# A two-layer decoder trunk: when the weights of the last feed-forward block are prepared, and three smaller reorderings

## The chip, the cores and the metric

The program runs on one core of a Trainium2 chip. Its engines are TensorE (PE: matmuls, with its weight loads listed apart as PEld), VectorE (DVE), ScalarE (ACT), GpSimd (POOL), and SyncE (SP), which here only issues transfers. Each works through its own queue in order; 16 DMA engines carry what SP, ACT and POOL issue. The metric is the time of one execution in microseconds (us) of device time. Three runs of the kernel before took 1037.97, 1039.06 and 1039.12 us: the median is 1039.06.

## The reference, cut to what matters

The input x has 256 rows (the sequence) of 1024 numbers; c is one row that conditions all. Two layers each do

```
x = x + 0.5 * gate0 * swiglu_ffn(pre(x, 0), w_in[i, 0], w_out[i, 0])
x = x + gate1 * mixer(pre(x, 1))            # layer 0: attention, layer 1: convolution module
x = x + 0.5 * gate2 * swiglu_ffn(pre(x, 2), w_in[i, 1], w_out[i, 1])
pre(z, j) = rms_norm(z, norm_g[i, j]) * (1 + scale_j) + shift_j
shift, scale, gate = (silu(c) @ ada_w[i] + ada_b[i]) cut into pieces
swiglu_ffn(h, w_in, w_out): a, b = split(h @ w_in); (silu(a) * b) @ w_out      # 2 x 2816 columns
```

The attention has 16 heads of 64, with q and k normalized by head, a distance penalty and a causal mask. The convolution module is

```
a, g = split(h @ w_pw1 + b_pw1); u = a * sigmoid(g)
u = depthwise causal convolution of width 31 over the rows, one filter for each of the 1024 channels
u = silu(layer_norm(u)) @ w_pw2 + b_pw2
```

All is float32: some 250 MB of weights are read once.

## The kernel before, in words

The 256 rows are two tiles, t = 0 and t = 1, of 128. Every large product is made in three matmuls (`mm3`, lines 680 to 682): each operand is a high part in a format that TensorE takes at full rate, and the rest as a low part; high x high, high x low and low x high are summed.

**The stream of weights.** All weights form one list, in the order of use, of pieces of 512 KB (`raw`), held in six buffers. `step()` takes the next piece: ACT copies the high part (`whi`, L251, one piece ahead), DVE subtracts it to get the low part (`wlo`, L226), the buffer comes free, and SP issues the load of the piece six places later (L211). Pieces of `ada_w` are instead summed up by DVE with the weights silu(c) (`acc`, L290 and L292). Two pieces are a unit, and high and low parts of six units fit (`RING`); a piece of a seventh is refused until the oldest unit has had its last use. Who calls `step()`: `need(unit)` until the unit is there; `block()` ahead of each group of matmuls, which adds a quota (`take(n)` sets it, about 1.6 to 1.8 here, 0 to stop) to a credit and steps as often as that holds a whole number; and explicit calls. As every queue is in order, the place of a `step()` in the program is its place among the other work of DVE and ACT.

**The feed-forward blocks** (`ffn`): for each of 11 chunks of 256 columns, U(t, c, u) makes the up products, `gate` silu(a) * b, `TR` turns it by transposes (L763) and splits it into gh and gl (L771, L772), and Dn(t, c) adds its part of the down product into y[t], two banks of 512 columns. `residual` (L614, L617) adds y to x, in the last block in pieces of 512, 256 and 256 columns, each stored at once. Between blocks `residual` also makes the norm: squares (ACT), a power (POOL), the scaled rows z (DVE); `turn` then transposes z (L659), applies scale and shift (hf, L665 and L667) and splits the result into hh and hl (L674, L675), which the next block's U products need.

**The start.** For each of four quarters q of the channels `early_sum` sums ada_w for the first scale and shift: one-column matmuls of acc (L544), sums of raw pieces (L554), a copy by ACT (`br`, L560), and one-column matmuls of it (L563); `early_transposes` turns the rows (L588). For q = 0 idle matmuls (L448) on constants fill waits.

**The attention** (`attention`): the order is written out in one list. U: q, k or v products; R, N, Q: norm of q and k and their transposes; S: scores of two heads (PE), penalty and row minimum (DVE L908), exponentials (ACT L914); M: division by the sum (DVE, L923 and L925); X: transposes of the result (PE, L932); V: product with v.

**The convolution** (`conv`): the channels are eight groups b of 128. U(b) makes the two halves, `glu(b)` multiplies them into a buffer ub (ACT L1085, DVE L1086). `park(b)` (POOL, L1095) writes ub to DRAM and `spread(b)` (POOL, L1103) reads it back in four transfers in a layout R in which 32 channels stand at four shifts; `wide(b)` (L1039) builds the matching filter matrix wd, on POOL or, for b of 6 and 7, on DVE. C(b) (L1111) is the depthwise product: 64 matmuls on R and wd, and a copy of the result by ACT (`v`, L1115). C(6) and C(7) are made in two halves, for the rows of t = 0 and of t = 1. `VT` transposes v, bn_stats and `norm` make the layer norm, `swish` and `put` the operand of O(t, j), the last product of the module, over four units of w_pw2. After it come `residual`, `turn` and the last feed-forward block. In the loop over b, `steps` says how many pieces are taken behind each C(b): 2, 2, 2 and 1 behind C(0) to C(3).

Of the kernel before, what the change touches and what calls it, by code (L numbers as in the profile page):

```python
# [14 lines left out]
P = 128  # L15
D = 1024
# [3 lines left out]
NC = DFF // 256  # L20
# [8 lines left out]
IDLE_START = 20  # L29
IDLE_SUMS = 2  # L30
IDLE_FOLD = 9
IDLE_PICK = 2
IDLE_FIRST = 12
MASKED = 1e30


# [22 lines left out]
class Trunk:  # L59
# [213 lines left out]
    def take(self, n=None):  # L273
        self.quota = PUMP[self.phase] if n is None else n
# [263 lines left out]
    def early_sum(self, q, acc, shift, idle):  # L538


        nc = self.nc
        def scale(ps):
            for i in range(2):
                nc.tensor.matmul(ps[:, i : i + 1], acc[:, i * P : i * P + P], self.one, start=True, stop=True)  # L544

        rows = self.bank("m" if q else "y")
        if not q:
            ps = self.bank("m")
            scale(ps)
        for e, raw in enumerate(shift):  # L550
            if not q and not e:
                idle(IDLE_SUMS)
            for k in range(4):
                nc.tensor.matmul(  # L554
                    rows[32 * k : 32 * k + 32, 0:256], self.sc32[:, 4 * e + k, :], raw[:, k, :],
                    start=e == 0, stop=e == 1,
                )
            self.issue()
        br = self.two.tile([P, 256], F32, name="br", tag="sq", bufs=1)
        nc.scalar.activation(br, rows[:, 0:256], AF.Copy)  # L560
        def shifts(ps):
            for i in range(2):
                nc.tensor.matmul(ps[:, 2 + i : 3 + i], br[:, i * P : i * P + P], self.pick, start=True, stop=True)  # L563

        if q:
            pt = self.early_transposes(q)
            ps = self.bank("m")
            scale(ps)
            shifts(ps)
        else:  # L570
            idle(IDLE_PICK)
            shifts(ps)
            pt = self.early_transposes(q)

        def fin():
            for j, kind in enumerate((1, 0)):
                self.finish(self.vecs[0, 0, kind], ps[:, 2 * j : 2 * j + 2], q * 256, 2)

        return fin, pt
# [112 lines left out]
            self.mm3(ps, self.hh[:, kk, ts], self.hl[:, kk, ts], unit.hi[:, cs], unit.lo[:, cs], kk == 0, kk == 7)  # L692
        unit.uses -= 1

    def rows256(self, y, lh, ll, unit, first, last, mid=None, quarters=False):


        self.need(unit)
        self.block()
        for h in range(2):  # L700
            if h and mid:
                mid()
            n = 256 if h and quarters else 512
            for o in range(0, 512, n):
                for k in range(2):
                    cs = slice(k * D + h * 512 + o, k * D + h * 512 + o + n)
                    self.mm3(
                        y[h][:, o : o + n], lh(k), ll(k), unit.hi[:, cs], unit.lo[:, cs],
                        first and k == 0, last and k == 1 and o + n == 512,
                    )  # L710
        unit.uses -= 1

    def bank(self, tag):
# [6 lines left out]
    def ffn(self, i, l, s, before, after, first=None, last=False, mid=None):  # L720
# [4 lines left out]
        up, down = p["up"], p["down"]  # L725
# [10 lines left out]
        def U(t, c, u):  # L736
            if u == 0:
                us[t, c] = self.bank("u")
            self.cols512(us[t, c], t, up[c][u], u)
            if u == 1:  # L740
                gate(t, c)
# [15 lines left out]
        def TR(c, ts=(0, 1)):  # L757
            ps = self.bank("m")
            g = gs[c]
            for j, t in enumerate(ts):  # L760
                for k in range(2):
                    o = (2 * j + k) * P
                    nc.tensor.transpose(ps[:, o : o + P], g[:, t, k * P : k * P + P], self.ident)  # L763
            if c not in gts:
                gts[c] = [
                    self.fp.tile([P, 2, 256], F32R, name=n, tag=n, bufs=3) for n in ("gh", "gl")
                ]
            n = len(ts)
            hi, lo = (gt[:, ts[0] : ts[0] + n, :] for gt in gts[c])
            src = ps[:, 0 : n * 256].rearrange("p (t n) -> p t n", t=n)  # L770
            nc.scalar.activation(hi, src, AF.Copy)  # L771
            nc.vector.tensor_tensor(lo, src, hi.bitcast(F32), op=ALU.subtract)  # L772

        def Dn(t, c, mid=None, quarters=False):
            if t not in y:
                y[t] = self.new_y()
            hi, lo = gts[c]
            self.rows256(
                y[t], lambda k: hi[:, t, k * P : k * P + P], lambda k: lo[:, t, k * P : k * P + P],
                down[c], c == 0, c == NC - 1, mid, quarters,  # L780
            )

        if first:
            self.take()
# [9 lines left out]
        else:  # L794
            take = self.take
# [8 lines left out]
        for c in range(6 if first else 2, e):  # L804
            U(0, c, 0), U(1, c, 0), TR(c - 1)
            if c == 7 and mid:
                mid()
            U(0, c, 1), U(1, c, 1)
            Dn(0, c - 1), Dn(1, c - 1)
        take = self.take  # L810
        U(0, e, 0), TR(e - 1), U(0, e, 1), Dn(0, e - 1), TR(e, (0,)), U(1, e, 0)
        self.need(down[e])
# [1 line left out]
        Dn(0, e)  # L814
        g2 = self.vecs[l, s, 2].out
        self.residual(0, y[0], g2, 0.5, last)
        take(0), U(1, e, 1), take(1), Dn(1, e - 1), TR(e, (1,))
        after()
        Dn(1, e, None, last)
        self.residual(1, y[1], g2, 0.5, last)  # L820


# [18 lines left out]
    def attention(self, ap, before, after):  # L841
# [3 lines left out]
        def U(t, units, u):  # L845
            if u == 0:
                us[t, id(units)] = self.bank("y")
            self.cols512(us[t, id(units)], t, units[u], u)
# [124 lines left out]
        U(1, A, 1), Q(0, 0), U(1, v0, 0), R(1, 0), U(1, v0, 1), N(1, 0)  # L973
        U(0, B, 0), Q(1, 0), W(1, 0), U(0, B, 1), S(0)
        U(1, B, 0), R(0, 1), M(0), U(1, B, 1), N(0, 1)
        U(0, C, 0), X(0), S(1), R(1, 1), Q(0, 1), U(0, C, 1), M(1), V(0), N(1, 1)
        U(1, C, 0), X(1), R(0, 2), Q(1, 1), U(1, C, 1), V(1), N(0, 2), S(2)
        U(0, E, 0), R(1, 2), Q(0, 2), M(2), U(0, E, 1), N(1, 2), X(2), S(3)
        U(1, E, 0), R(0, 3), Q(1, 2), V(2), M(3), U(1, E, 1), N(0, 3), X(3), S(4)
# [40 lines left out]
    def conv(self, cp, before, after):  # L1020
# [71 lines left out]
        def park(b):  # L1092

            drams[b] = self.dram.tile([P, 288], F32, name=f"d{b}")
            nc.gpsimd.dma_start(drams[b], ub[b % 4])  # L1095
# [107 lines left out]
        take(PUMP_LOOP)  # L1203
        U(4)
        glu(4)
        steps = (2, 2, 2, 1, 0, 0)
        for b in range(4):
            if b < 3:
                U(b + 5)
            if b == 0:  # L1210
                take(0)
            park(b + 4), spread(b + 3)
            if b:
                wide(b + 2)
            if b < 3:
                glu(b + 5)
            C(b)
            for _ in range(steps[b]):
                self.step()
            if b:  # L1220
                VT(b - 1)
                if b == 1:
                    nc.vector.tensor_tensor(b2, b2, gate, op=ALU.mult)
                else:
                    x = self.x[b - 2]
                    nc.vector.tensor_tensor(x, x, b2, op=ALU.add)
        nc.scalar.activation(warm, self.mhalf, AF.Silu)
        spread(7), wide(6, nc.vector)
        C(4)
        for _ in range(steps[4]):  # L1230
            self.step()
        VT(3), wide(7, nc.vector)
        C(5)
        for _ in range(steps[5]):
            self.step()
        VT(4), C(6, 0, P), VT(5), take(4), self.block(), C(7, 0, P), VT(6, (0,))
        take(0)
        C(6, P, P), VT(7, (0,)), moments(0), norm(0, 0), norm(0, 1)
# [66 lines left out]
```

## Time and profile before

| | us |
|---|---|
| median of three runs | 1039.06 |
| the profiled execution | 1036.53 |
| its span, first to last instruction | 1034.7 |
| PE, PEld busy | 1016.2, 824.0 |
| DVE, ACT, POOL busy | 785.9, 490.1, 71.3 |
| mean granted TensorE clock | 0.997 of full |

Times are counted from the first instruction. A busy PE in the table is not a PE at its peak: matmuls overlap, and the ends are modelled. So the stretches in which the next matmul waits for another engine, and their releaser, say more than the share. The stages in this execution: the start to about 60 us, the first feed-forward block to 228, the attention to 337, two feed-forward blocks to 735, the convolution with its last product to 842, the last block to the end.

### The profile page before, as it was taken

What the parts mean: (1) busy time and instruction counts of PE and PEld (TensorE: products, weight loads), DVE (VectorE), ACT (ScalarE), POOL (GpSimd) and SP (SyncE); (2) the same over time, 40 slices, a digit from 0 to 9 for tenths busy, and PEclk for the clock granted to TensorE, in tenths of its full rate; (3) what the DMA queues carried; (4) which work ended last, traced back from release to release, by engine and by line L of the source; (5) the groups of instructions that cost most, each with busy time, mean ns of one, the idle gap of its engine ahead of it and who ended that gap; (6) DMA issues with size and microseconds to landing.
All of it is one profiled execution on the core that took longest, in us unless ns stands there. A gap on an engine that the chain in (4) does not pass through costs nothing.

```text
span 1034.7 us, 14612 instructions
## 1 busy us (share of the span) xinstructions
PE 1016.2 (98%) x5457; PEld 824.0 (80%) x5457; DVE 785.9 (76%) x1167; ACT 490.1 (47%) x762; POOL 71.3 (7%) x123
## 2 busy tenths in 40 slices
PE   9999999999999999999999999999999899999998
PEld 6788787887676888887888887888986788888886
DVE  5779888988897788878778778786788578656633
ACT  4554344566575544444455444354534356444420
POOL 3000000002210000000020000000166000000000
PEclk9999999999999999999999999999999899999999
DMA  9989999948665399999839889886599238766601
GB/s 334 331 272 340 315 328 322 321 145 274 233 216 194 107 328 318 298 318 306 298 101 310 287 301 302 286 291 198 173 279 312 97 104 304 233 214 218 219 32 41
DMA packets 183754, 256.08 MB, mean 247 GB/s; under 512 B 9045, under 2 KB 132726, under 8 KB 183684
## 3 DMA queue, kind: packets, MB, share of 16 engines
q1 hardware_dynamic: 180928, 248.55, 72.3%
q0 software_dynamic: 2608, 6.55, 2.3%
q8 instruction: 43, 0.70, 0.3%
q14 instruction: 27, 0.22, 0.1%
q10 hardware_dynamic: 148, 0.06, 0.0%
HBM read 252.89 MB, written 2.23 MB: 247 GB/s over the span
## 4 chain that ended last, share of the span: by engine, by line
PE 86%; DVE 7%; ACT 3%; DMA 3%; issue 1%; POOL 0%; SPq 0%; DVEq 0%; ACTq 0%; POOLq 0%
PE u L682 15%; PE u L680 15%; PE u L681 15%; PE y L680 11%; PE y L682 11%; PE y L681 11%; PE m L1111 2%; DVE wlo L226 2%; PE m L763 2%; DVE acc L292 2%; DMA raw<-in_ada_w_dram 1%; DMA R<-d 1%; ACT whi L251 1%; ACT p L914 1%; DMA raw<-in_attn_w_qkv_dram 1%
## 5 line engine op out<-in xcount | busy, mean ns | idle before, releaser
L226 DVE TENSOR_TENSOR wlo<-raw,whi 128x1024 fp32r<-128x1024 f32 x320 | 386.0, 1235 | 32.4 <-ACT whi L251 32.3
L251 ACT ACTIVATE whi<-raw 128x1024 fp32r<-128x1024 f32 x320 | 329.3, 1055 | 155.5 <-DMA raw<-in_ffn_w_in_dram 73.0
L680 PE MATMUL u<-whi,hh 128*128 128x512 f32 x672 | 266.3, 396 | 0.0
L682 PE MATMUL u<-whi,hl 128*128 128x512 f32 x672 | 262.8, 391 | 0.1
L681 PE MATMUL u<-wlo,hh 128*128 128x512 f32 x672 | 261.8, 390 | 0.2 <-DVE wlo L226 0.2
L292 DVE SCALAR_TENSOR_TENSOR acc<-raw,sc,acc 128x512 f32<-128x512 f32 x224 | 172.2, 769 | 5.1
L682 PEld LDWEIGHTS u<-whi,hl 128*128 128x128 f32 x672 | 126.1, 188 | 29.1 <-DVE hl L604 1.4
L680 PEld LDWEIGHTS u<-whi,hh 128*128 128x128 f32 x672 | 126.2, 188 | 26.2 <-issue 0.8
L681 PEld LDWEIGHTS u<-wlo,hh 128*128 128x128 f32 x672 | 126.4, 188 | 25.7 <-DVE wlo L226 0.6
L680 PE MATMUL y<-whi,gh 128*128 128x512 f32 x354 | 138.5, 391 | 0.7 <-ACT gh L771 0.7
L682 PE MATMUL y<-whi,gl 128*128 128x512 f32 x354 | 137.6, 389 | 0.0
L681 PE MATMUL y<-wlo,gh 128*128 128x512 f32 x354 | 137.4, 388 | 0.0
L772 DVE TENSOR_TENSOR gl<-m,gh 128x512 fp32r<-128x512 f32 (+1 forms) x48 | 31.0, 647 | 88.9 <-ACT gh L771 88.7
L680 PE MATMUL y<-whi,hh 128*128 128x512 f32 (+1 forms) x256 | 96.7, 378 | 1.5 <-DVE hh L1164 0.8
L682 PE MATMUL y<-whi,hl 128*128 128x512 f32 (+1 forms) x256 | 93.9, 367 | 0.0
L681 PE MATMUL y<-wlo,hh 128*128 128x512 f32 (+1 forms) x256 | 93.6, 366 | 0.0
L771 ACT ACTIVATE gh<-m 128x512 fp32r<-128x512 f32 (+1 forms) x48 | 27.0, 563 | 135.2 <-PE m L763 135.1
L733 ACT ACTIVATE sg<-u 128x256 f32<-128x256 f32 x84 | 32.1, 383 | 110.4 <-PE u L682 110.4
L680 PEld LDWEIGHTS y<-whi,gh 128*128 128x128 f32 x354 | 66.5, 188 | 16.3 <-ACT gh L771 1.4
L682 PEld LDWEIGHTS y<-whi,gl 128*128 128x128 f32 x354 | 66.5, 188 | 14.5 <-DVE gl L772 0.6
L681 PEld LDWEIGHTS y<-wlo,gh 128*128 128x128 f32 x354 | 66.5, 188 | 13.4
L680 PEld LDWEIGHTS y<-whi,hh 128*128 128x128 f32 x256 | 48.7, 190 | 12.5 <-issue 3.5
(178 smaller groups left out, 881.7 us busy)
## 6 DMA issues: line engine op xcount, KB each, us to landing
raw<-in_ffn_w_in_dram SPq DMA_DIRECT2D x164, 512.0 KB, 5.2
raw<-in_ada_w_dram SPq DMA_DIRECT2D x144, 512.0 KB, 5.0
raw<-in_ffn_w_out_dram SPq DMA_DIRECT2D x88, 512.0 KB, 5.1
raw<-in_attn_w_qkv_dram SPq DMA_DIRECT2D x24, 512.0 KB, 5.1
raw<-in_conv_w_pw_dram SPq DMA_DIRECT2D x24, 512.0 KB, 6.1
raw<-in_ffn_w_in_dram SPq DMA_DIRECT2D x24, 256.0 KB, 4.7
R<-d POOLq DMA_DIRECT2D x32, 142.0 KB, 7.3
raw<-in_attn_w_o_dram SPq DMA_DIRECT2D x8, 512.0 KB, 4.2
```

The costliest lines, as they stand in the source:

```text
L226: (eng or nc.vector).tensor_tensor(lo, raw, hi.bitcast(F32), op=ALU.subtract)
L251: self.nc.scalar.activation(hi, self.like(self.raws[i], hi), AF.Copy)
L292: nc.vector.scalar_tensor_tensor(dst, raw[:, i, :], self.sc[:, k : k + 1], dst, op0=ALU.mult, op1=ALU.add)
L680: nc.tensor.matmul(out, lh, rh, start=start, stop=False)
L681: nc.tensor.matmul(out, lh, rl, start=False, stop=False)
L682: nc.tensor.matmul(out, ll, rh, start=False, stop=stop)
L733: nc.scalar.activation(sg, ps[:, 0:256], AF.Silu)
L763: nc.tensor.transpose(ps[:, o : o + P], g[:, t, k * P : k * P + P], self.ident)
L771: nc.scalar.activation(hi, src, AF.Copy)
L772: nc.vector.tensor_tensor(lo, src, hi.bitcast(F32), op=ALU.subtract)
L914: nc.scalar.activation(p[:, c0:c1], p[:, c0:c1], AF.Exp, bias=st[:, t : t + 1], scale=-1.0, accum_out=st[:, 2 + t : 3 + t],)
L1111: nc.tensor.matmul(ps[32 * g : 32 * g + 32, :], wd[b][:, q, g, :], R[b][:, g, 4 * q + t0 : 4 * q + t0 + n], start=q == 0, stop=q == 7,)
```

## The change

There are four parts. **Convolution**: the list `steps` is gone; no piece is taken behind C(0) to C(3), two are taken behind C(5) instead. `wide(4)` stands on POOL ahead of park(6) and spread(5) instead of behind them. **Last feed-forward block**: the down products of t = 1 for the last three chunks are made by columns. The second 512 columns of chunk 8 are left for the end, then the first 512 columns are finished, and the second 512 in two pieces of 256 with the last two chunks each. **Attention**: M(1) stands right behind S(1), ahead of R(1,1), Q(0,1) and U(0,C,1), instead of behind them. **Start**: for q = 0 the transposes stand ahead of the one-column matmuls of br, in place of two idle matmuls, and 8 instead of 12 idle matmuls follow.

```diff
-IDLE_PICK = 2
-IDLE_FIRST = 12
+IDLE_FIRST = 8
...
+        pt = self.early_transposes(q)
         if q:
-            pt = self.early_transposes(q)
             ps = self.bank("m")
             scale(ps)
-            shifts(ps)
-        else:
-            idle(IDLE_PICK)
-            shifts(ps)
-            pt = self.early_transposes(q)
+        shifts(ps)
...
+        def Dp(c, o, n, last=False):
+            hi, lo = gts[c]
+            self.need(down[c])
+            for k in range(2):
+                cs, gs_ = slice(k * D + o, k * D + o + n), slice(k * P, k * P + P)
+                self.mm3(
+                    y[1][o // 512][:, o % 512 : o % 512 + n], hi[:, 1, gs_], lo[:, 1, gs_],
+                    down[c].hi[:, cs], down[c].lo[:, cs], False, last and k == 1,
+                )
...
-            Dn(0, c - 1), Dn(1, c - 1)
+            Dn(0, c - 1)
+            if last and c == e - 1:
+                Dp(e - 2, 0, 512)
+            else:
+                Dn(1, c - 1)
...
-        take(0), U(1, e, 1), take(1), Dn(1, e - 1), TR(e, (1,))
-        after()
-        Dn(1, e, None, last)
+        take(0), U(1, e, 1), take(1)
+        if last:
+            Dp(e - 1, 0, 512), TR(e, (1,)), Dp(e - 2, 512, 512), Dp(e, 0, 512, True)
+            for o in (512, 768):
+                Dp(e - 1, o, 256), Dp(e, o, 256, o == 768)
+        else:
+            Dn(1, e - 1), TR(e, (1,))
+            after()
+            Dn(1, e)
...
-        U(0, C, 0), X(0), S(1), R(1, 1), Q(0, 1), U(0, C, 1), M(1), V(0), N(1, 1)
+        U(0, C, 0), X(0), S(1), M(1), R(1, 1), Q(0, 1), U(0, C, 1), V(0), N(1, 1)
...
-        steps = (2, 2, 2, 1, 0, 0)
         for b in range(4):
             if b < 3:
                 U(b + 5)
             if b == 0:
                 take(0)
+            if b == 2:
+                wide(4)
             park(b + 4), spread(b + 3)
-            if b:
+            if b in (1, 3):
                 wide(b + 2)
             if b < 3:
                 glu(b + 5)
             C(b)
-            for _ in range(steps[b]):
-                self.step()
...
         C(5)
-        for _ in range(steps[5]):
-            self.step()
+        self.step(), self.step()
         VT(4), C(6, 0, P), VT(5), take(4), self.block(), C(7, 0, P), VT(6, (0,))
```

## Rows read from the trace of the kernel before

**Rows 1.** The page, part 1: busy us, share of the span, instructions by engine.

```profile
PE 1016.2 (98%) x5457; PEld 824.0 (80%) x5457; DVE 785.9 (76%) x1167; ACT 490.1 (47%) x762; POOL 71.3 (7%) x123
```

**Rows 2.** Windows by stage; after each engine's busy us: PEclk, DMA share, GB/s.

```profile
790.00:815.00 25.00, 20.14 (x411) 14.75 (x411) 15.74 (x17) 8.28 (x13) 6.57 (x10) 0.93 0.82 247
815.00:835.00 20.00, 19.21 (x88) 15.73 (x88) 12.13 (x30) 9.03 (x22) 1.10 (x2) 0.91 0.00 1
835.00:862.00 27.00, 27.00 (x128) 22.35 (x127) 22.57 (x35) 17.48 (x30) 0.55 (x1) 1.00 0.51 165
900.00:950.00 50.00, 50.00 (x228) 41.32 (x227) 29.93 (x34) 20.77 (x26) 0.00 (x0) 1.00 0.68 219
```

**Rows 3.** Timeline of PE, last depthwise products: start, duration, [idle before <- releaser].

```profile
798.93 1.96 PE L1111 MATMUL m<-R,wd 128*32 128x128 f32 x64 [0.75 <-DMA R<-d]
...
805.36 2.77 PE L1111 MATMUL m<-R,wd 128*32 128x128 f32 x64 [4.10 <-DMA R<-d]
...
811.27 1.95 PE L1111 MATMUL m<-R,wd 128*32 128x128 f32 x64
...
816.99 0.80 PE L680 MATMUL y<-whi,hh 128*128 128x512 f32 x1 [0.79 <-DVE hh L1164]
```

**Rows 4.** Timeline of POOL, 764 to 798 us.

```profile
782.68 0.60 POOL L1095 DMA_DIRECT2D d<-ub  x1 [1.78 <-DMA d<-ub]
...
787.50 0.60 POOL L1095 DMA_DIRECT2D d<-ub  x1
...
791.69 2.12 POOL L1039 TENSOR_TENSOR wd<-w,mask 128x1024 f32<-128x1024 f32 x1
795.29 2.21 POOL L1103 DMA_DIRECT2D R<-d  x4 [1.48 <-issue]
```

**Rows 5.** Tile R, then loads by line (KB, median us to landing), 740:815 and 860:1000.

```profile
DMA to landing us min/median/max: 5.4/7.3/9.4
...
raw<-in_ffn_w_in_dram SPq DMA_DIRECT2D x8, 512.0 KB, 14.2
...
raw<-in_ffn_w_in_dram SPq DMA_DIRECT2D x31, 512.0 KB, 5.0
```

**Rows 6.** Window 817 to 820 us, columns as in Rows 2.

```profile
817.00:820.00 3.00, 3.00 (x7) 2.42 (x8) 2.90 (x8) 1.71 (x5) 0.13 (x1) 0.50 0.00 0
```

**Rows 7.** Timeline of DVE from O(0,3) to the first chunk, then PE's there.

```profile
829.25 0.69 DVE L614 SCALAR_TENSOR_TENSOR tmp<-y,gate 128x512 f32<-128x512 f32 x1 [1.76 <-PE y L682]
...
836.50 1.37 DVE L665 TENSOR_SCALAR hf<-m,mod,mod 128x128 f32<-128x128 f32 x4 [0.61 <-PE m L659]
...
840.21 3.49 DVE L226 TENSOR_TENSOR wlo<-raw,whi 128x1024 fp32r<-128x1024 f32 x3
843.61 0.68 DVE L614 SCALAR_TENSOR_TENSOR tmp<-y,gate 128x512 f32<-128x512 f32 x1
...
854.43 0.50 PE L682 MATMUL u<-whi,hl 128*128 128x512 f32 x1
```

**Rows 8.** Timeline of ACT and of PE's weight loads at the start.

```profile
25.78 1.06 ACT L251 ACTIVATE whi<-raw 128x1024 fp32r<-128x1024 f32 x1 [0.25 <-DMA raw<-in_ffn_w_in_dram]
...
28.47 0.19 PEld L680 LDWEIGHTS u<-whi,hh 128*128 128x128 f32 x1 [0.33 <-ACT hh L603]
```

**Rows 9.** Timeline of PE and DVE in the attention, around M(1) and X(1).

```profile
267.25 1.27 PE L932 MATMUL m<-ident,p 128*128 128x128 f32 x6 [1.70 <-DVE p L925]
...
263.23 0.69 DVE L856 TENSOR_REDUCE s<-sq 128x8 f32<-128x512 f32 x1 [1.51 <-ACT sq L853]
...
267.93 0.68 DVE L864 TENSOR_TENSOR z<-y,r 128x512 f32<-128x512 f32 x1
```

**Rows 10.** Timeline of PE and DVE at the end of the kernel.

```profile
1026.97 0.50 PE L680 MATMUL y<-whi,gh 128*128 128x512 f32 x1 [0.47 <-ACT gh L771]
...
1030.18 0.42 DVE L614 SCALAR_TENSOR_TENSOR tmp<-y,gate 128x256 f32<-128x256 f32 x1
...
1031.56 0.42 DVE L617 TENSOR_TENSOR x<-x,tmp 128x256 f32<-128x256 f32 x1
```

More of the change, by code (lines that the diff above doesn't have):

```diff
@@ L693, in cols512, with rows256 @@
         unit.uses -= 1
-    def rows256(self, y, lh, ll, unit, first, last, mid=None, quarters=False):
+    def rows256(self, y, lh, ll, unit, first, last, mid=None):
         self.need(unit)
@@ L702, in rows256 @@
                 mid()
[L703 to L710, printed above, removed]
+            for k in range(2):
+                cs = slice(k * D + h * 512, k * D + h * 512 + 512)
+                self.mm3(y[h], lh(k), ll(k), unit.hi[:, cs], unit.lo[:, cs], first and k == 0, last and k == 1)
         unit.uses -= 1
@@ L772, in TR, with Dn @@
             nc.vector.tensor_tensor(lo, src, hi.bitcast(F32), op=ALU.subtract)
-        def Dn(t, c, mid=None, quarters=False):
+        def Dn(t, c, mid=None):
             if t not in y:
@@ L779, in Dn @@
                 y[t], lambda k: hi[:, t, k * P : k * P + P], lambda k: lo[:, t, k * P : k * P + P],
-                down[c], c == 0, c == NC - 1, mid, quarters,
+                down[c], c == 0, c == NC - 1, mid,
             )
+        def Dp(c, o, n, last=False):
+            hi, lo = gts[c]
+            self.need(down[c])
+            for k in range(2):
+                cs, gs_ = slice(k * D + o, k * D + o + n), slice(k * P, k * P + P)
[3 more added lines that the diff above has]
+                )
         if first:
@@ L1229, in conv @@
         C(4)
-        for _ in range(steps[4]):
-            self.step()
         VT(3), wide(7, nc.vector)
         C(5)
-        for _ in range(steps[5]):
-            self.step()
+        self.step(), self.step()
         VT(4), C(6, 0, P), VT(5), take(4), self.block(), C(7, 0, P), VT(6, (0,))
```

## The prediction, made before the changed kernel ran

> **What bounds the kernel now.** First the busy shares: PE is busy for 98% of the span, DVE for 76% [rows 1]. That says where to look, not what a stage waits for, so next the windows by stage. In the last block, 900 to 950 us, PE runs without a gap, 228 matmuls in 50 us or 0.22 us each, and DVE is idle for 40% of it: PE alone sets the pace, and whatever comes late or early there is passed to the end unchanged [rows 2]. The end of the convolution, 790 to 815, is different: PE is busy for 20.1 of 25 us and its clock is 0.93 of full. Behind it, 815 to 835, no DMA moves at all and DVE is idle for 7.9 of 20 us; from 835 to 862 DVE is busy for 22.6 of 27 [rows 2]. Third, the timeline of PE in the bad stretch: C(6) for t = 0 waits 0.75 us for R, C(7) for t = 0 waits 4.10 us, and then 64 matmuls take 2.77 instead of 1.95 us, because the clock has fallen [rows 3]. So this stage is bound by the last spread, not by PE. I follow what each part does to the start of O(0,0), now at 816.99, and then to the stages behind it.
>
> **Convolution, the depthwise products.** The chain that ends last is POOL's. park(6) is issued at 782.68 after POOL was idle for 1.78, so POOL was free at 780.9; park(7) goes out at 787.50; wide(5) ends at 791.69 + 2.12 = 793.81; spread(7), which needs the landing of d(7), starts at 795.29, 7.8 us after park(7) [rows 4]. Afterwards wide(4) starts at 780.9, in that idle time, and park(6) behind it at about 783.0, 0.3 late. park(7) no longer has wide(4) ahead of it and its input no longer stands behind DVE's pieces: 785.7, 1.8 early. With the same 7.8 us d(7) has landed by 793.5; wide(5) still ends near 793.8. So spread(7) starts at about 793.8, 1.5 early. Its last transfer went out three quarters through the four, at 796.95, and PE started at 805.36, 8.4 later. A transfer of R took 5.4 at best, 7.3 in the middle and 9.4 at worst, while a load of 512 KB beside it took 14.2 against 5.0 in the last block [rows 5]: the two share the engines. With the loads gone (six stay in flight until about 787) I take the best value: 793.8 + 1.65 + 5.4 + 0.2 = 801.0. C(6), without its wait, would let PE go on at 800.4, so C(7) starts at 801.0.
>
> From there: three half products of 1.9 at full clock and two pairs of transposes of 0.2 end at about 807.2 (before: 805.36 to 811.27 + 1.95 = 813.22). In this time ACT meets four copies of weight pieces ahead of its copy of C(7); at 1.06 each they end about when PE needs it, and I charge 0.1. From the end of the last half product to O(0,0) it was 816.99 - 813.22 = 3.8 [rows 3], the same work after: O(0,0) at 811.1, **5.9 us earlier**. Ends: if R stays as slow as before (8.4), C(7) starts at 803.9 and the gain is 3.1; with no wait at all it is 6.5.
>
> **The clock.** Between 817 and 820 PE made 7 matmuls in 3.00 us at 0.50 of the clock, 0.43 each, against 0.22 [rows 2, 6]: 7 x 0.21 = 1.5 us, say 1.4. That fall came after 3.8 us of narrow products and transposes, with only 0.79 of idle time [rows 3]. The same work stands ahead of O(0,0) afterwards. Whether the clock falls again depends on when the chip looks, which one trace can't show: 0 or 1.4, I take **0.7 gained**. The Trainium skill ("TensorE: Matmul & The Clock Gate", section "Why this matters for your kernels") ties a return to the lower level to idle gaps of PE between bursts of matmuls. By that rule nothing would fall here afterwards and the term would be 1.4; the row, a fall with next to no gap, speaks for 0; the middle stands.
>
> **The pieces that were put off.** Five of the seven pieces of `steps` now come later: they fall into the O stage, where before the ring of six units was full and no piece could be taken. Counting the credits with 1.6 for each group of O: two pieces ahead of O(0,2), one ahead of O(0,3), two ahead of O(1,0), one, two and two ahead of the next three. So by the end of the module 21 pieces are done, against 20 before, and the first sum of ada_w also comes one group sooner. A piece is 1.16 us of DVE (3.49 for three) [rows 7]. Where do they stand? Three between the last `put` and residual(0): DVE was idle 1.76 there, until 829.25, so residual(0) moves by 3.5 - 1.8 = 1.7. Three instead of one ahead of hf at 836.50, where 0.61 was idle: hf moves by 1.7 + 2.3 - 0.6 = 3.4, of which the wait for hh takes up some 0.6: 2.8. Four instead of three ahead of residual(1), which followed the pieces without a gap (840.21 + 3.49, 843.61): 2.8 + 1.2 = 4.0. Then z, the transposes, hf and hl of t = 1 follow, with the early sum of ada_w another 0.3: 4.3 to 4.5. PE needed that hl at 854.43, when it was just there, its matmul lengthened to 0.50 [rows 7]. So PE loses **4.4 us**, in pieces at O(0,3), the transposes of t = 1 and U(1,0,0). Ends: 0, if five pieces (5.8) fit into the 7.9 idle us [rows 2]; 8.1, if seven stand on the path in full. The chain in rows 7 is in order and had no slack at its end, so I take the worked value. The loads behind these pieces find idle DMA engines [rows 2] and cost nothing; were they as slow as 14.2 [rows 5], rival B would hold.
>
> **Start.** Six idle matmuls less, at 0.23 some 1.4 us of PE, let the first products begin up to 0.7 earlier (they then wait for hh and hl of the first quarter). But in the second quarter ACT waits for a load until 25.78, and its copy of 1.06 stands ahead of hf and hh, for which PE waits at 28.47 [rows 8]. PE only waits longer: **0**. Ends: 0.7 gained; 1.4 lost if the thinner start costs the clock one fall.
>
> **Attention.** X(1) waits 1.70 for M(1) [rows 9]. Put behind S(1), M(1) falls into the 1.51 us in which DVE waits for ACT's square at 263.23, and pushes that a little. What is late next is z at 267.93, which stood behind M(1) and which the next transposes need as soon as X(1) ends, 267.25 + 1.27; it moves by the length of M(1), about 1.3, less 0.3. I take **1.0**; ends 0 (DVE waits for the exponentials as long as it gained) and 1.7.
>
> **Tail.** The wait of 0.47 for gh goes, since twelve other matmuls lie between TR and its use, and the first matmul's restart (0.50 for 0.23) with it; six matmuls of 512 columns become twelve of 256, about 0.07. Behind the last matmul DVE needs 1030.18 to 1031.56 + 0.42, 1.80 us for four operations [rows 10]. Both pieces lie in one bank, and residual stands behind all their matmuls, so I take it that this stays: **0.7** gained. Ends 0.5 and, if the first piece needn't wait, 1.7. The deferral of chunk 8 itself moves no work off PE.
>
> **Sum.** 5.9 + 0.7 - 4.4 + 0 + 1.0 + 0.7 = 3.9 us. The profiled execution took 1036.53 (span 1034.7 and 1.8 around it): 1032.6. The median of the runs is 2.5 higher, 1039.06, and is what is compared: **1035.2**.
>
> **Rivals.**
> A. The put-off pieces are absorbed: DVE finds the idle time in front of each step of the chain, 4.4 becomes 0. Time 1035.2 - 4.4 = 1030.8. For it: 7.9 idle us between 815 and 835. Against: that idle time lies ahead of waits on PE, in order, and 835 to 862 has only 4.4 [rows 2].
> B. A load stands in ACT's queue. The copy of the sixth piece after the two steps behind C(5) needs a load that is issued only at about 798, and ACT's copy of C(7) stands behind it. I reckon with 5 us [rows 5]; at 7.4 it is 2.4 late, and so is O(0,0): 1037.6.
> C. The slower side: spread(7) isn't freed. If R(7) is paced by its own small packets and by the landing of d(7), C(7) starts near 805 as before, 5.9 and the 0.7 of the clock are gone, and the put-off pieces are paid all the same: 1035.2 + 6.6 = 1041.8. It decides from a start of C(7) at about 804. For it: the median of 7.3 is the same while loads come and go. Against: the spread of 5.4 to 9.4 [rows 5]. The Trainium skill ("DMA: Bandwidth & Descriptors", "Queues, rings and completion order") has each DMA engine take turns between the queues that have work; by that rule an empty load queue must shorten R, and C would fail.
>
> **How the numbers follow.** Two runs of this kernel can't be told apart within some 0.2%, 2.1 us. My forecast, a loss of 3 to 6 at the pieces and C(7) before 802, holds 1032.5 to 1037.0: chance 0.46. A 0.16, B 0.14, C 0.13; 0.11 is left for small terms that leave it within 0.2%. Faster: 0.46 + 0.16 = 0.62; same: 0.14 + 0.11 = 0.25; slower 0.13. The range from 1030.5 to 1039.5 takes in A, B and the bounds of the small terms, and leaves out most of C and what is faster than A.
>
> **What would show it.** PE's wait ahead of C(7) under 1 us and no clock below full before 807; R landing in about 5.4; O(0,0) about 7 us earlier by the trace's own count (5.9 and the attention's 1.0). Then new waits of PE between O(0,3) and U(1,0,0), 4.4 in sum, with DVE's wlo or hl as releaser, and none before that. X(1) without a wait, Q(1,1) with one under 1 us. The first product of the second quarter still waiting for hh at 28.5. The last matmul 1.8 us ahead of the last DVE operation. It is wrong if O(0,0) comes less than 4 us earlier, or if PE passes U(1,0,0) without a wait.

## The result

The change is faster: 1030.55 us (median of 4 runs, 1029.38 to 1031.33) against 1038.57 for the kernel before in the same comparison, a ratio of 0.9927 with an interval of 0.9914 to 0.994. A second comparison, later and on another set of runs, gave 1030.52 against 1036.79, 0.9944 (0.9924 to 0.9964). The profiled execution of the change took 1031.33, its span is 1029.6.

Part 1 of the page of the change, which answers to [rows 1]:

```profile
PE 1013.7 (98%) x5457; PEld 821.8 (80%) x5457; DVE 781.1 (76%) x1167; ACT 488.9 (47%) x762; POOL 70.5 (7%) x123
```

The shares are what they were. The windows by stage, set some 7 us earlier than in [rows 2] and with the same columns (PE, PEld, DVE, ACT, POOL, then PEclk, DMA share, GB/s), show where it changed; the last row answers to [rows 6]:

```profile
783.00:808.00 25.00, 24.80 (x519) 17.02 (x512) 15.21 (x19) 10.25 (x16) 9.28 (x15) 1.00 0.64 189
808.00:828.00 20.00, 19.21 (x85) 15.45 (x84) 14.29 (x30) 10.73 (x24) 0.80 (x2) 0.91 0.32 103
828.00:855.00 27.00, 25.21 (x117) 20.05 (x117) 23.55 (x36) 17.21 (x29) 0.84 (x2) 1.00 0.55 184
...
810.00:813.00 3.00, 3.00 (x8) 2.33 (x9) 2.90 (x9) 1.48 (x5) 0.00 (x0) 0.50 0.03 10
```

In the first stage PE is busy for 24.8 of 25 us instead of 20.1, with the clock at full. In the third it now idles for 1.8 us where it had not idled at all: that is the larger part of the 2.8 us lost to the pieces put off (table below). The clock still falls behind O(0,0).

The timeline of PE at the last depthwise products, then POOL's, then what waits in the O stage (start, duration, [idle before <- releaser]); they answer to [rows 3], [rows 4] and the end of [rows 7]:

```profile
775.29 0.44 PE L1136 MATMUL y<-ident,v 128*128 128x128 f32 x2 [1.34 <-ACT v L1126]
...
797.24 1.96 PE L1122 MATMUL m<-R,wd 128*32 128x128 f32 x64
...
799.49 1.95 PE L1122 MATMUL m<-R,wd 128*32 128x128 f32 x64
...
809.77 0.74 PE L675 MATMUL y<-whi,hh 128*128 128x512 f32 x1 [0.79 <-DVE hh L1175]
...
844.36 1.10 PE L654 MATMUL m<-ident,z 128*128 128x128 f32 x8 [0.70 <-DVE z L638]
...
849.29 0.50 PE L675 MATMUL u<-whi,hh 128*128 128x512 f32 x1 [1.09 <-ACT hh L669]
```

```profile
775.68 0.56 POOL L1106 DMA_DIRECT2D d<-ub  x1 [7.96 <-DVE ub L1097]
776.23 2.18 POOL L1114 DMA_DIRECT2D R<-d  x4
778.43 3.79 POOL L1050 TENSOR_TENSOR wd<-w,mask 128x1024 f32<-128x1024 f32 x2
782.16 0.60 POOL L1106 DMA_DIRECT2D d<-ub  x1
...
784.92 0.56 POOL L1106 DMA_DIRECT2D d<-ub  x1
...
787.67 1.92 POOL L1050 TENSOR_TENSOR wd<-w,mask 128x1024 f32<-128x1024 f32 x1
789.53 2.20 POOL L1114 DMA_DIRECT2D R<-d  x4
```

C(6) and C(7) for t = 0 follow one another without a wait; before, C(7) waited 4.10. spread(7) starts at 789.53, 4.6 us behind park(7) at 784.92, where it was 7.8, and its four transfers landed in 2.87 to 3.11 us. At 775.29 PE waits 1.34 for v(0), which stands on ACT behind copies of pieces that wait for loads; the first profile of before has no such wait, but two others with the old convolution have it (1.12 in e12, 1.89 in e2). The landing times of all transfers of R, answering to [rows 5]:

```profile
DMA to landing us min/median/max: 2.9/6.3/9.8
```

The stages of fourteen executions can be set beside each other, since PE's matmuls come in the same order. The table takes the start of the same matmul in two traces; each number is what an execution gained in that stage on the first profile of the kernel before (minus: lost). "Start" is up to 228.07 in that profile, "attention" from there to 285.61, "to O(0,0)" from there to 816.99, "O stage" to 855.92, "tail" the rest; "more" is how many more pieces than before stand on DVE between O(0,0) and residual(1), "fall" whether the clock falls behind O(0,0). The first profile had that fall too; the same kernels with it and without it differ by 1.4 to 1.6 us in the O stage, so only rows with the same entry under "fall" show there what the pieces cost.

| execution | start | attention | to O(0,0) | O stage | more | fall | tail |
|---|---|---|---|---|---|---|---|
| before, again (e8) | 0.28 | 0.65 | -0.18 | 0.10 | 0 | yes | 0.01 |
| attention only (e12) | -0.25 | 1.82 | -0.75 | 1.47 | 0 | no | 0.01 |
| the rest only (e2) | 0.90 | 1.16 | -2.48 | 0.02 | 0 | yes | 0.75 |
| wide(4) only (e3) | -0.05 | 1.67 | -1.68 | 1.42 | 0 | no | 0.75 |
| **the change** | 0.67 | 1.53 | 5.03 | -2.81 | 5 | yes | 0.75 |
| the change, again (e9) | 0.21 | 1.73 | 3.06 | -1.25 | 5 | no | 0.75 |
| convolution only (e1) | -0.05 | -0.67 | 6.10 | -2.64 | 5 | yes | -0.02 |
| steps only (e4) | 0.74 | 1.75 | 5.82 | -1.28 | 5 | no | 0.76 |
| traffic (e5) | 0.22 | 1.71 | 2.45 | -2.74 | 5 | yes | 0.44 |
| after C(4) (e6) | 0.77 | 1.36 | 3.95 | -0.07 | 2 | yes | 0.73 |
| take(0) (e7) | -0.22 | 1.81 | 4.63 | -3.94 | 6 | yes | 0.74 |
| pieces early (e10) | 1.02 | 1.74 | 5.32 | 1.45 | 2 | no | 0.75 |
| the same, old order (e11) | 0.63 | 1.62 | 5.11 | -0.12 | 2 | yes | 0.73 |

For the change the row sums to 5.2, which is 1036.53 - 1031.33. The medians lie 8.0 apart in the first comparison and 6.3 in the second; on that below.

### The profile page after: what moved, and what is told of

Same layout as the page of the kernel before. It is cut to its first block, busy times and chain, and to the rows that moved or that the text cites. A ratio compares the mean times of both kernels' runs of the same rounds, so it can differ in the third digit from the quotient of the medians.

```text
span 1029.6 us, 14614 instructions
## 1 busy us (share of the span) xinstructions
PE 1013.7 (98%) x5457; PEld 821.8 (80%) x5457; DVE 781.1 (76%) x1167; ACT 488.9 (47%) x762; POOL 70.5 (7%) x123
## 4 chain that ended last, share of the span: by engine, by line
PE 82%; DVE 8%; ACT 4%; issue 3%; DMA 3%; POOL 0%; SPq 0%; POOLq 0%; DVEq 0%; ACTq 0%
PE u L677 15%; PE u L675 14%; PE u L676 14%; PE y L675 10%; PE y L677 10%; PE y L676 10%; DVE wlo L225 2%; DVE acc L291 2%; PE m L753 2%; PE m L1122 2%; ACT whi L250 1%; DMA raw<-in_conv_w_pw_dram 1%; ACT p L925 1%; DMA raw<-in_ffn_w_in_dram 1%; DMA raw<-in_attn_w_qkv_dram 1%
## 5 line engine op out<-in xcount | busy, mean ns | idle before, releaser
L675 PE MATMUL y<-whi,gh 128*128 128x512 f32 (+1 forms) x356 | 138.9, 390 | 0.2 <-ACT gh L761 0.2
L677 PE MATMUL y<-whi,gl 128*128 128x512 f32 (+1 forms) x356 | 137.9, 387 | 0.0
L676 PE MATMUL y<-wlo,gh 128*128 128x512 f32 (+1 forms) x356 | 137.8, 387 | 0.0
```

Of the source, the lines that this page charges most:

```text
L675: nc.tensor.matmul(out, lh, rh, start=start, stop=False)
L676: nc.tensor.matmul(out, lh, rl, start=False, stop=False)
L677: nc.tensor.matmul(out, ll, rh, start=False, stop=stop)
```

## The experiments

**The change in two halves.** e1 is the kernel before with the convolution part alone (`steps` gone, two steps behind C(5), wide(4) ahead). 

> The kernel before with the convolution part of the change alone. Theory: the part gives 5.0 us up to O(0,0) and pays 2.5 back to the pieces put off, as the two profiles put side by side say: 2.5 faster, ratio 0.9976, PE's C(7) for t = 0 without a wait, and U(1,0,0) later against O(0,0) by 2.5. Rival (the medians lie 8.0 apart, the two profiles only 5.2, and the missing 2.8 belong to this part): 5.3 faster, ratio 0.995.

 Measured: 1033.36 against 1037.34, ratio 0.996 (0.9947 to 0.9973), between the two; the interval takes in the rival's 0.995 and not the theory's 0.9976. Its trace has no wait ahead of C(7) and loses 2.64 in the O stage, as expected; in this execution the clock also fell in the attention:

```profile
266.70 1.27 PE L932 MATMUL m<-ident,p 128*128 128x128 f32 x6 [1.69 <-DVE p L925]
...
270.18 0.63 PE L680 MATMUL y<-whi,hh 128*128 128x512 f32 x1
```

A matmul of 512 columns takes 0.63 instead of 0.39 there, behind the same wait that the profile of before passed at full clock [rows 9]. e2 is the change with the old convolution. 

> The change without its convolution part: start, attention and tail. Theory: 0.65 + 1.54 + 0.75 = 2.9 us, ratio 0.9972, with PE's wait of 4.1 ahead of C(7) back. Rival (the missing 2.8 us between medians and profiles lie in the start, where one profile can hide a slower one): 5.7, ratio 0.9945.

 Measured: 1032.92 against 1037.34, ratio 0.9964 (0.9951 to 0.9978); here the interval takes in the theory's 0.9972 and not the rival's 0.9945. So what the medians show beyond the profiles belongs more to the convolution than to the rest. The two halves, 4.0 and 3.6 per thousand by their ratios, add up to about what the whole gave in the first comparison (7.3; in the second it was 5.6). C(7) waits for R again, and the clock falls behind it:

```profile
804.95 3.64 PE L1122 MATMUL m<-R,wd 128*32 128x128 f32 x64 [3.84 <-DMA R<-d]
```

**Which half of the convolution part.** e3 is the change with `steps` as before. So it differs from e2 only in the place of wide(4):

```diff
+            if b == 2:
+                wide(4)
             park(b + 4), spread(b + 3)
-            if b:
+            if b in (1, 3):
                 wide(b + 2)
```

> The change with the list steps put back: pieces are taken behind C(0) to C(3) again, none behind C(5), and only the order of wide(4) on POOL differs in the convolution. Theory (pieces and their loads are what held up R): R keeps a median of 7 us, spread(7) comes 1.5 to 2 earlier than before and no more, C(7) waits 2 to 3 us, no backlog is paid: 2.9 + 1.5 = 4.4 faster than before, ratio 0.9958. Rival (POOL's order was the whole of it): C(7) without a wait and no backlog: 7.9 faster, ratio 0.9924, as fast as or faster than the change.

 Measured: 1037.33 against 1037.34, ratio 0.9997 (0.9984 to 1.0011): both theories missed. By the ratios the move alone eats all that start, attention and tail give (e2, 0.9964). DVE, POOL and PE in that trace:

```profile
777.12 5.29 DVE L225 TENSOR_TENSOR wlo<-raw,whi 128x1024 fp32r<-128x1024 f32 x1 [1.51 <-ACT whi L250]
```

```profile
777.54 3.79 POOL L1050 TENSOR_TENSOR wd<-w,mask 128x1024 f32<-128x1024 f32 x2
783.11 0.60 POOL L1106 DMA_DIRECT2D d<-ub  x1 [1.78 <-DVE ub L1097]
...
791.08 4.11 POOL L1050 TENSOR_TENSOR wd<-w,mask 128x1024 f32<-128x1024 f32 x1
795.13 2.21 POOL L1114 DMA_DIRECT2D R<-d  x4
```

```profile
795.24 5.35 PE L1122 MATMUL m<-R,wd 128*32 128x256 f32 x64 [2.79 <-POOL wd L1050]
```

While POOL makes two filter matrices in a row, one wlo of DVE takes 5.29 instead of 1.22; ub(6) and with it park(6) wait for that, and wide(5), beside DVE's next operations, takes 4.11 instead of 1.93 and is now what C(5) waits for. spread(7) starts at 795.13: hardly earlier than before (795.29), though the stages ahead had gained 1.6. The Trainium skill ("SBUF — State Buffer", "Who interferes with whom") has DVE operations with two SBUF inputs and POOL operations that read SBUF shut each other out of a shared pair of ports for a whole instruction; these rows agree.

They show the blocking, but not its whole price. The profiled execution took 1034.38, 3 us less than the median of its twelve runs, and up to O(0,0) it is no worse than e2's, which was the slowest of its six. What differs over all runs is the mean granted clock: its median is 0.994 in e3 and 0.997 in e2. At the 0.8 us for each 0.001 that is worked out further down, that is some 2.4 of the 4.4 us between their medians.

e4 is the reverse: `steps` gone, wide(4) where it was. 

> The change with wide(4) put back behind park(6) and spread(5); steps stays removed. Theory: R lands in 3 to 4 us, R(7) lands some 5 us before it is needed after the change, so two us of POOL cost nothing: the same as the change, ratio 0.9927 within 0.001. Rival (the order matters): park(7) goes out 1.9 later and C(7) waits again, 1 to 2 us slower than the change.

 Measured: 1029.7 against 1037.34, ratio 0.993 (0.9918 to 0.9942), the same as the change.

```profile
790.66 2.21 POOL L1114 DMA_DIRECT2D R<-d  x4
```

spread(7) does go out 1.4 us later than in the change, once what the stages ahead had gained (2.5 and 2.2) is taken off, but R(7) lands at 796.47, still 1.9 ahead of C(7). So all that the convolution part gives in time comes from the pieces that are no longer taken; the order of wide(4) is worth nothing without them and, by e3 and e2, harmful with them.

**Traffic or queues?** e5 is the change with the transfers of `steps` put back without their copies:

```diff
...
             C(b)
+            nc.sync.dma_start(scr[b : b + 1, :], us["v", b][0:1, 0:8])
+            for i in range((2, 2, 2, 1)[b]):
+                j = 2 * b + i
+                nc.sync.dma_start(dum[j], a["ffn_w_in"][1, 1, 0:512, 256 * j : 256 * j + 256])
```

> The change, with seven transfers of 512 KB put into SP's queue behind C(0) to C(3), two, two, two and one, each behind a small transfer that waits for the copy of its C; they go from a weight to unused DRAM and nobody waits for them. It adds the traffic that steps stood for without the pieces on ACT and DVE. Theory (the traffic makes R slow): the last transfers of R take 6 to 8 us again instead of 3, d(7) lands at about 791.5 instead of 787.8, spread(7) starts there, R(7) lands near 801, and C(7) for t = 0 waits 1 to 2.5 us: 1 to 4 us slower than the change. Rival (the pieces' place in the queues of ACT and DVE was what held things up): R slower by less than 2 us, no wait, the same time as the change within 0.1%.

 Measured: 1033.43 against 1035.83, ratio 0.9975 (0.9963 to 0.9988), 3 to 5 us slower than the change by the ratios. The first theory held in its mechanism:

```profile
784.81 0.56 POOL L1108 DMA_DIRECT2D d<-ub  x1
789.76 2.18 POOL L1116 DMA_DIRECT2D R<-d  x4 [4.39 <-DMA d<-ub]
...
793.81 2.20 POOL L1116 DMA_DIRECT2D R<-d  x4
```

```profile
801.81 1.95 PE L1124 MATMUL m<-R,wd 128*32 128x128 f32 x64 [1.60 <-DVE wlo L225]
```

park(7) leaves at 784.81 as in the change, but d(6) and d(7) take 7 us, spread(7) goes out at 793.81, and R(7) landed after 5.5 to 6.0 us at 801.46, 0.35 ahead of C(7). (The releaser that the row names had long been done; the landing of R is what came last.) Up to O(0,0) it gains 2.45. The three profiles with the change's convolution gain 4.7 there on the mean, the four with the old one -0.9: traffic alone takes back some 2.3 of 5.6 us. spread(7) starts as late as before (793.81, against 795.29 less the 1.9 that the stages ahead have gained), so traffic alone is enough to make the chain of d and spread as late as it was. R itself lands faster than the 7.4 to 8.1 that R(7) took before. The copy of the traffic is not exact: its transfers go out from 775.5 to 791.5, the loads before from 782.0 to 799.5, so two or three instead of four or five are in flight beside R(7); and they end in DRAM, not in SBUF. Whether that is all of the other half, or the pieces' place in the queues of ACT and DVE has a share, was not tried.

**The backlog.** e6 is the change with three pieces more, behind C(4). 

> The change, with three pieces more taken behind C(4). Their data lie in the buffers since 784, ACT and DVE have nothing else there, and their loads go out when R(7) is already issued. Theory (the pieces put off cost 2.5 us in the O stage, by one piece of 1.16 each on DVE's chain): three fewer in the backlog, U(1,0,0) loses 0 to 0.5 us against O(0,0) instead of 2.5: 2 to 2.5 us faster than the change, ratio 0.9905. Rival (the loss behind O(0,0) is not the number of pieces but the chain of residual, turn and hl itself): no gain, ratio 0.993.

 Measured: 1030.77 against 1035.83, ratio 0.9949 (0.993 to 0.9968): in time nearer to the rival's 0.993 than to the theory's 0.9905, in the trace the theory's. Two more pieces instead of five stand in the O stage and nothing is lost there (-0.07); but the gain is spent earlier:

```profile
803.56 1.06 ACT L250 ACTIVATE whi<-raw 128x1024 fp32r<-128x1024 f32 x1 [1.58 <-DMA raw<-in_ffn_w_in_dram]
```

```profile
804.93 0.33 PE L1136 MATMUL y<-ident,v 128*128 128x128 f32 x1 [2.25 <-ACT v L1126]
```

That is rival B's mechanism, in this kernel and not in the change: a copy that waits for its load stands on ACT ahead of v(7), and PE waits 2.25 ahead of VT(7).

e7 puts take(0) ahead of U(5), against the wait of 1.34 at 775.29. 

> The change, with take(0) ahead of U(5) instead of behind it: U(5) takes no pieces ahead of need, so ACT's sg(5) and v(0) no longer stand behind five copies that wait for loads. Theory: PE's wait of 1.34 us ahead of VT(0) goes and park(5) leaves 8 to 10 us earlier; one piece more is put off (up to 1.16): 0.2 to 1.4 us faster than the change. Rival (U(6) or U(7) waits for its weights instead, since the loads set the pace there): same or up to 1 us slower.

 Measured: 1033.51 against 1035.83, ratio 0.9981 (0.9967 to 0.9996), and the rival was right, with more loss than it said: PE's wait for v(0) is gone, but U(7) waits 1.07 for wlo of its own weights, and six more pieces in the O stage cost 3.94. (U(6) waits 0.80, but 0.66 to 0.74 in e6, e8 and e11 too.)

**Two kernels again.** e8 is the kernel before. 

> The kernel before, unchanged, for a second profile of it. Theory (the medians lie 8.0 apart and the two profiles 5.2 because executions of the kernel before differ in how often the clock falls): the starts of its stages agree with the first profile within 0.5 us, except for steps of 1.4 us at falls of the clock, in other number than the two of the first profile. Rival (the difference lies in waits for transfers): other steps, with a DMA as releaser and the clock at full.

 Measured: 1035.49 against 1035.83. Its stages agree with the first profile within 0.65, and C(7) waits 3.70. The clock falls at the same two places, behind C(7)'s wait for longer than in the first profile; no wait for a transfer differs by more than 0.7. It shows the 2.8 us of neither theory. e9 is the change. 

> The change itself, unchanged, to have it beside the next kernels on one chip, and for a second profile. Expected: 1029 to 1032 us, no wait of PE ahead of C(6) and C(7) for t = 0, and 2.4 us lost between O(0,0) and U(1,0,0) against the kernel before.

 Measured: 1030.52 against 1036.79. No wait at C(6) or C(7), but 2.45 at VT(0) and a fall of the clock behind it, and none behind O(0,0). The loss in the O stage is 1.25 against the first profile; against e12 and e3, whose clock did not fall there either (1.47, 1.42), it is 2.7, as in the change's first profile. Both rows have the columns of the windows above:

```profile
776.00:779.00 3.00, 2.97 (x17) 2.97 (x18) 1.75 (x3) 0.71 (x2) 2.58 (x5) 0.62 1.01 399
812.00:815.00 3.00, 3.00 (x14) 2.35 (x15) 2.90 (x8) 1.71 (x5) 0.12 (x1) 1.00 0.04 16
```

**Pieces early.** e10 is the change with nine pieces ahead of O(0,0), put where their data lie ready:

```diff
             C(b)
+            if b == 3:
+                self.step(), self.step()
...
         C(4)
+        self.step(), self.step()
...
-        VT(4), C(6, 0, P), VT(5), take(4), self.block(), C(7, 0, P), VT(6, (0,))
+        VT(4), C(6, 0, P), VT(5), take(3), self.block(), C(7, 0, P), VT(6, (0,))
```

> The change, with the pieces put where ACT and DVE have nothing else to do and their data lie ready: two behind C(3), two behind C(4), two behind C(5), and three instead of four in the block behind VT(5), nine instead of six before O(0,0). Theory (each piece in the backlog costs its 1.16 us of DVE in the O stage, and a piece costs nothing where its load has landed and R(7) is issued): U(1,0,0) loses 0 to 0.5 us against O(0,0) instead of 2.4, and the wait of 2.25 us that the run with three pieces behind C(4) had ahead of VT(6) falls below 0.5: 2 us faster than the change. Rival (the loads of the first two pieces meet R(7), as steps did): R(7) lands after 799 and C(7) waits; no gain.

 Measured: 1027.34 against 1036.79, ratio 0.9912 (0.9895 to 0.9929), on the same chip as e9's 1030.52: 3.2 us better than the change (six runs each; the two intervals just overlap). PE and DVE in that trace:

```profile
798.90 1.96 PE L1122 MATMUL m<-R,wd 128*32 128x128 f32 x64 [0.56 <-DMA R<-d]
```

```profile
817.90 2.36 DVE L225 TENSOR_TENSOR wlo<-raw,whi 128x1024 fp32r<-128x1024 f32 x2
...
825.58 1.22 DVE L225 TENSOR_TENSOR wlo<-raw,whi 128x1024 fp32r<-128x1024 f32 x1
...
830.70 3.49 DVE L225 TENSOR_TENSOR wlo<-raw,whi 128x1024 fp32r<-128x1024 f32 x3
```

Two, one and three pieces stand ahead of residual(0), hf and residual(1), against none, one and three before. The first two exceed DVE's idle 1.76 us [rows 7] by 0.6, the idle 0.61 ahead of hf takes that up, and the chain is not late. C(7) waits 0.56 for R, as the first loads meet R(7): its four transfers took 2.80 to 6.61, against 2.87 to 3.11 in the change. e11 is the same with wide(4) where it was before the change. 

> The same places for the pieces, with wide(4) put back behind park(6) and spread(5). Theory (the order of wide(4) is worth nothing once the loads are gone): the same time as the run before it within 0.1%. Rival (spread(7) goes out a microsecond later and meets the first loads): C(7) waits 0.5 to 2 us and it is that much slower.

 Measured: 1027.99 against 1036.79, ratio 0.9914 (0.9897 to 0.993), the same as e10. The rival's wait came (C(7) waits 0.88, 0.32 more than in e10), but a difference of time can't be told from the spread of the runs.

**Attention alone.** e12 is the kernel before with M(1) behind S(1). 

> The kernel before with M(1) right behind S(1), and nothing else. Theory: X(1) loses its wait of 1.70, Q(1,1) gets one of about 1.5 for z, X(1) itself is shorter, and with 0.4 at S(1) the attention ends 1.5 us earlier: ratio 0.9985. Rival (in executions whose clock falls behind X(1)'s wait, as one profile showed, 1.4 us more go): ratio 0.997.

 Measured: 1034.18 against 1036.79, ratio 0.998 (0.9966 to 0.9994), which holds both. From the last matmuls ahead of X(1) to Q(1,1) it gains 1.2.

## Why the prediction was right, and where it was not

The direction, the place and the exchange were right: a gain at C(7), a smaller loss at the pieces, small gains elsewhere. The size was not: the gain was forecast as 3.9 and measured as 8.0 and 6.3. 1030.55 lies below the 1032.5 to 1037.0 of the likeliest case and 0.05 above the lower end of the range, which was luck.

Of the 4.6 us by which the time of 1035.2 missed, 1.3 lie in the terms: they sum to 3.9, the two profiles differ by 5.2. The other 3.3 came in with the last step of the sum. It added to the changed kernel the 2.5 us by which the median of the kernel before lies above its profile, without a reason why they should stay; the median of the change lies 0.8 below its profile. More on this at the end of the section. The terms one by one:

- **C(7) and O(0,0): forecast 5.9, measured 5.0** in the pair of profiles. Over the three profiles with this convolution (5.03, 3.06, 6.10) and the four with the old one (0, -0.18, -0.75, -2.48) the means differ by 5.6. The size was right, two steps inside it were not. That wide(4) frees spread(7) by letting park(7) go 1.8 earlier failed: less the 2.2 us that the stages ahead had gained, park(6) went out 1.7 late and park(7) only 0.4 early. spread(7) came 3.6 early all the same (forecast 1.5), as d(7) landed in 2.92 instead of 7.25; e3 and e4 show that the pieces' absence does it. And R took 3.0 alone, not the 5.4 that was the best of a stretch in which loads never ceased [rows 5]; R(7) landed 5.2 us before it was needed, so C(7) had no wait at all. That surplus bought nothing, since PE was the limit by then. The wait at VT(0) was not forecast; it comes and goes in both kernels and took 1.34 here, 2.45 in e9, nothing in the first profile of before. The Trainium skill ("DMA: Bandwidth & Descriptors", "Queues, rings and completion order") has each DMA engine take turns between the queues that have work; 3.0 without the loads and 5.5 to 6.0 beside the transfers of e5 agree with that.
- **The clock: forecast 0.7, measured 0.** It fell again at O(0,0). In the fourteen executions it fell there in nine, in both kernels; the middle was a fair price for a toss, and the change does not touch it.
- **The pieces: forecast -4.4, measured -2.8.** The chain was priced well: residual(0) 1.7 late (forecast 1.7), hf 3.3 (3.4). The count failed: the step "four instead of three ahead of residual(1)" made six more pieces on the chain, though the text itself put off five. There were three, and residual(1) was 2.8 late, not 4.0 (times against O(0,0)):

```profile
820.31 3.49 DVE L225 TENSOR_TENSOR wlo<-raw,whi 128x1024 fp32r<-128x1024 f32 x3
823.72 0.68 DVE L609 SCALAR_TENSOR_TENSOR tmp<-y,gate 128x512 f32<-128x512 f32 x1
...
832.53 1.36 DVE L660 TENSOR_SCALAR hf<-m,mod,mod 128x128 f32<-128x128 f32 x4
...
835.81 3.49 DVE L225 TENSOR_TENSOR wlo<-raw,whi 128x1024 fp32r<-128x1024 f32 x3
839.22 0.68 DVE L609 SCALAR_TENSOR_TENSOR tmp<-y,gate 128x512 f32<-128x512 f32 x1
```

  The new waits were not the ones that were named, for wlo or hl, 4.4 in sum: PE waits 0.70 for z and 1.09 for hh, and the rest goes in steps of 0.1 to 0.2 around these waits, behind a first wlo and behind O(0,0). In e7, which does have six more, the loss is 3.9. Two more cost nothing, five 2.8, six 3.9: behind the idle time each piece costs about its length.
- **Start: forecast 0, measured about 0.5.** The ten executions with the new start stand between -0.22 and 1.02, mean 0.5; the four with the old one between -0.25 and 0.28, mean 0. The step that failed is that ACT waits for a load at 25.78 whatever comes before [rows 8]. In the change's first profile the two copies run through, as the second load landed 0.9 earlier; in its second profile (e9) ACT waits as forecast:

```profile
24.02 1.99 ACT L250 ACTIVATE whi<-raw 128x1024 fp32r<-128x1024 f32 x2
```

```profile
25.58 1.06 ACT L250 ACTIVATE whi<-raw 128x1024 fp32r<-128x1024 f32 x1 [0.68 <-DMA raw<-in_ffn_w_in_dram]
```

  So the mean hides two cases. In six of the ten the copies run through and the start gains 0.63 to 1.02; in four (e3, e5, e7, e9) ACT waits 0.63 to 0.74 and it gains -0.22 to 0.22, as the four with the old start, which all wait. Why the load lands early in one execution and not in the next isn't shown. The 0.67 of the first profile lies just within the bound of 0.7 that was given.
- **Attention: forecast 1.0, measured 1.1 to 1.2** at M(1) itself, from the last matmuls ahead of X(1) on. The wait for z that was named as next late came, larger than "under 1 us":

```profile
264.31 0.82 PE L943 MATMUL m<-ident,p 128*128 128x128 f32 x6
266.58 0.63 PE L887 MATMUL m<-ident,z 128*128 128x128 f32 x4 [1.46 <-DVE z L875]
```

  X(1) itself is 0.45 shorter (0.82 for 1.27). The 0.4 more in the pair of profiles came ahead of it, at a wait for kT that the second profile of before doesn't have either.
- **Tail: forecast 0.7, measured 0.75**, in every execution with it but one (0.44). DVE's four operations still stand behind the last matmul and take 1.8, as both pieces wait for the end of their bank [rows 10]:

```profile
1024.70 0.28 PE L677 MATMUL y<-whi,gl 128*128 128x256 f32 x1
```

```profile
1025.02 0.42 DVE L609 SCALAR_TENSOR_TENSOR tmp<-y,gate 128x256 f32<-128x256 f32 x1 [1.45 <-PE y L677]
...
1026.39 0.42 DVE L612 TENSOR_TENSOR x<-x,tmp 128x256 f32<-128x256 f32 x1
```

Of the rivals, A's time (1030.8) came true without its mechanism, since the pieces were not absorbed; it takes nine of them ahead of O(0,0), as in e10. B didn't occur in the change. C fell: C(7) started at 799.49.

What is left is the rest of the difference. The pair of profiles differs by 5.2; with the means above (0.5 + 1.2 + 5.6 - 2.8 + 0.75) it is 5.3, and the medians say 6.3 and 8.0. An execution without a profile doesn't show where it waits, but the mean granted clock of every run in the later comparisons is on record, and most of the rest goes with it. In 64 runs of the kernel before the time falls with the clock (correlation -0.88): a line through them gives some 0.8 us for each 0.001, and the median is 1037.4 at 0.995 and 1035.2 at 0.997. The first profile of the kernel before had 0.997, more than the mean of 0.9952 in the second comparison; the change had 0.998 in its profile and 0.9983 in the mean. At 0.8 us, the clock makes 2.5 of the 6.3 us there and 0.8 of the 5.2 between the profiles, and in both some 4 us are left.

Why the change's runs have the higher clock is not shown. The kernel before waits longer in more places, and a long wait was often followed by a fall of the clock, at some 1.4 us each; in e1 the wait at X(1), which the change removes, had one, in two other executions it had none. That fits, but no run took the waits away and kept all else.

## What to carry to other kernels

Work that prefetches for a later stage is not free because its engines look idle: it pays in the latency of the transfers beside it, in the queues that it stands in, and, moved later, in the chain that it then stands on. Before putting it off, count per queue position how many pieces stand ahead of each step and how many fit into the idle time there; the best place here was between, where its data have landed and the urgent transfers are already issued (e10, 3.2 us better than the change). And compare stages of several executions rather than two totals: the two profiles of the change differed by 2.0 us up to O(0,0) and by 1.6 in the O stage. Where a profile stands for a median, look whether its granted clock is that of the other runs.

## What the hardware showed that was not expected

A fall of the granted clock (to 0.50, the lower of its two levels, 1.2 GHz, for a few us) cost 1.4 to 1.6 us and came at the same places in some executions and not in others. Ahead of O(0,0) PE had idled 0.79 in all fourteen; behind it the clock fell in nine and not in five. In the convolution, PE's waits of 1.89, 2.27, 2.45, 2.79, 3.70, 3.84, 4.10 and 4.31 were followed by a fall, those of 1.07 to 1.60 and one of 2.25 were not; at X(1) 1.69 was, 1.65 and 1.70 were not. The Trainium skill ("TensorE: Matmul & The Clock Gate", "Why this matters for your kernels") ties the fall to idle gaps between bursts: the long waits agree, the falls behind O(0,0) don't. The second surprise is the mutual blocking of DVE and POOL in e3: 5.29 for an operation of 1.22, and 4.11 for one of 1.93. The kernel before has it too: at 778.81 one wlo takes 3.17 beside wide(3) on POOL.
